# Up product of an encoder layer: groups of three tiles, two of them by seven products, and weight forms in pieces of 1024 columns

## The chip, the cores and the metric

The kernel runs on one core of a Trainium2 chip. A time is the device time of one execution in microseconds; the kernel before has a median of 783.61 us over 3 runs (783.21 to 783.69). The profile is one execution recorded by the hardware profiler. PE is TensorE (matmuls), PEld its weight loads, DVE VectorE, ACT ScalarE, POOL GpSimd, SP SyncE.

## The reference

One layer for 512 tokens of width 1024, in float32:

```python
x1 = x  + RMSNorm_post_mix( W_out( sig(a_ret) * W_ret_o(Retention(h)) + sig(a_sgu) * W_sgu_o(SGU(h)) ) )
y  = x1 + RMSNorm_post_ffn( ConvGatedMLP( RMSNorm_pre_ffn(x1) ) )

def _conv_gated_mlp(h, w_up, conv_w, conv_b, w_down):
    hid = h @ w_up                      # (512, 1024) @ (1024, 2 * 2816)
    hid = conv(hid, conv_w) + conv_b    # each channel by itself, 3 tokens
    a, b = jnp.split(hid, 2, axis=-1)
    return (jax.nn.gelu(a) * b) @ w_down
```

(`conv` stands for the reference's call of the library.) The change is mostly in `h @ w_up`, the up product.

## The kernel before

**Precision.** Every product is made of float32 values split into a high and a low part (`split`: ACT copies to a rounded type, DVE subtracts, L119). Three matmuls stand for one: high by high, high weight by low activation, low weight by high activation.

**The up product.** `w_up` has 2 x 2816 columns, which are 22 tiles of 128 channels of `a` with the 128 of `b` that belong to them. A tile computed whole is two blocks (`f_block`), one for `a` and one for `b`: 8 pieces of 128 rows, three matmuls of 512 columns (the tokens) each, 24 matmuls into one bank of PSUM. A tile by seven products (`Pair`) treats its 2 x 2 submatrices by a Strassen form: seven products of 12 matmuls of 256 columns (`product`, L926), 84 in place of 8 x 12. For these the weights are added in forms first (`w_form`: T1 to T4 from B11, B12, B21, B22), and so are the activations (S1 to S4, made once). `part1` makes four products (B11 and B21, then T1 by S1 and T2 by S2), `part2` one (T3 by S3), `part3` the last two (T4 and B22). They use three banks: the first product's bank is copied out by ACT (`copy(two(c0[:, T0]), o)`) before the fourth product is written to it, and ACT copies the fourth and fifth too; DVE adds the second, fifth's partner and last. The last is the subtraction at L976, which completes the tile.

Tiles 0 to 3 are whole. `COUPLES` are (4, 5) to (18, 19): the first tile of each by seven products, the second whole, one inside the other. 20 and 21 are whole. `tile_done` makes the convolution of a finished tile (`conv`: one ACT operation L1247, two of DVE, L1250 and L1254, for each of its two parts), then `gated` (GELU on ACT L1261, a product on DVE L1263), and after tiles 7, 9, 11, 13 and 17 the forms of the down product's activations (`down_forms`: `fs`, `fa`, `fh`, `fl`; some of their low parts come by an adding transfer on POOL's queue, L1273).

**Weights.** All weights lie in `wall`, in pieces of 128 x 1024 (512 KB). SP starts a piece's transfer to a `raw` tile (4 buffers), ACT and DVE split it into slots of the pool `w4` (9 buffers of 1088 columns). A whole block takes two slots, high and low; a form of a seven-product tile is 512 columns and has its high and low part in one slot. `units` lists the pieces in the order of use, `w_get` hands out the next and prepares those behind it while they fit in nine slots (`w_size`).

**The order.** Each engine executes its instructions in the order in which a scheduler put them when the program was built; it starts from the order in the code and from its own view of times, and may move an instruction past others. What waits for a semaphore holds up all that stands behind it on its engine.

The seven-product kind is also used for two other stages: the products U and G (four pairs each, order in `MIDDLE`) and four gated pairs (`gated_pair`). The pairs of those stages use the same `w_form`; for G and the gated pairs T2 and T4 are added by POOL (`eng`), else by DVE.

## Time and profile before

| | before |
|---|---|
| median of the runs | 783.61 us |
| span of the profiled execution | 782.6 us |
| busy PE / DVE / ACT / POOL | 774.5 / 639.5 / 485.2 / 103.5 us |
| matmuls | 5139 |
| transfers `raw<-wall` by SP's queue | 144, 512 KB each, 3.7 us from issue to landing |
| software queue (POOL's transfers) | 14.95 MB, 9.0% of 16 engines' span |

The profiled execution's own time is the span of 782.6 us, and what lies around the span in the runs is 783.61 - 782.6 = 1.0 us. The up product from its first couple is the stretch from about 490 to 639 us. The page divides the span into 40 slices of 19.6 us; busy tenths of an engine in each show which engine is full where:

```profile
PE   9999999999999999999999999999999999999996
DVE  6567987789789988877765679989999889886987
ACT  7555568688466766644454686657777568644542
POOL 0040001130021102033211200001111012200001
```

The up product's couples are slices 26 to 33.

### The profile page before, as it was taken

How to read it: one execution, taken by the hardware profiler on the slowest of the kernel's cores; microseconds unless marked ns; L12 is line 12 of the kernel's file. 1: busy time of each engine (PE TensorE's matmuls, PEld its weight loads, DVE VectorE, ACT ScalarE, POOL GpSimd, SP SyncE). 2: the span in 40 equal slices, each digit the busy share in tenths (PEclk: the TensorE clock that was granted, in tenths of full speed). 3: DMA queues.
4: the chain of work that ended last, by engine and by line, in shares of the span. 5: the costliest groups of instructions: out<-in, count | busy, mean ns of one | idle time of the engine just before them, and what ended most of it. 6: DMA issues, size and time to landing. Idle time of an engine off the chain costs nothing.

```text
span 782.6 us, 13472 instructions
## 1 busy us (share of the span) xinstructions
PE 774.5 (99%) x5139; PEld 720.7 (92%) x5139; DVE 639.5 (82%) x1093; ACT 485.2 (62%) x878; POOL 103.5 (13%) x132
## 2 busy tenths in 40 slices
PE   9999999999999999999999999999999999999996
PEld 8888998998999999999998998999999998999996
DVE  6567987789789988877765679989999889886987
ACT  7555568688466766644454686657777568644542
POOL 0040001130021102033211200001111012200001
PEclk9999999999999999999999999999999999999998
DMA  8783224453223233233459120435555375733344
GB/s 288 271 246 102 81 82 162 108 122 108 81 91 126 82 122 121 83 110 106 138 171 337 54 81 28 124 107 141 142 148 149 108 199 111 171 114 107 109 162 162
DMA packets 35889, 104.80 MB, mean 134 GB/s; under 512 B 4400, under 2 KB 6320, under 8 KB 35824
## 3 DMA queue, kind: packets, MB, share of 16 engines
q1 hardware_dynamic: 27936, 87.81, 34.0%
q0 software_dynamic: 7024, 14.95, 9.0%
q10 hardware_dynamic: 864, 1.18, 0.4%
q8 instruction: 40, 0.66, 0.4%
q14 instruction: 25, 0.20, 0.1%
HBM read 91.34 MB, written 4.19 MB: 122 GB/s over the span
## 4 chain that ended last, share of the span: by engine, by line
PE 92%; DVE 3%; DMA 3%; issue 1%; ACT 0%; POOLq 0%; DVEq 0%; POOL 0%; ACTq 0%
PE ps L926 24%; PE ps L300 12%; PE ps L302 12%; PE ps L301 12%; PE ps L1372 7%; PE ps L755 5%; PE ps L634 4%; PE ps L636 4%; PE ps L635 4%; DMA raw<-wall 3%; PE ps L1109 2%; PE ps L1108 2%; PE ps L1107 2%; DVE dl L119 1%; PE ps L997 1%
## 5 line engine op out<-in xcount | busy, mean ns | idle before, releaser
L119 DVE TENSOR_TENSOR wl<-raw,wh 128x1024 fp32r<-128x1024 f32 (+1 forms) x84 | 96.0, 1152 | 54.3 <-issue 19.1
L100 ACT ACTIVATE wf<-raw 128x512 fp32r<-128x512 f32 x140 | 85.6, 625 | 67.3 <-PE ps L301 19.4
L926 PE MATMUL ps<-sh,wf 128*128 128x256 f32 x640 | 117.4, 276 | 0.1
L119 DVE TENSOR_TENSOR wf<-raw,wf 128x512 fp32r<-128x512 f32 x140 | 107.0, 774 | 9.2 <-ACT wf L100 8.6
L926 PEld LDWEIGHTS ps<-sh,wf 128*128 128x128 f32 x640 | 101.9, 192 | 1.1 <-ACT sig L100 0.5
L100 ACT ACTIVATE wh<-raw 128x1024 fp32r<-128x1024 f32 (+2 forms) x88 | 84.8, 977 | 28.5 <-DMA raw<-wall 14.0
L300 PE MATMUL ps<-h2h,wh 128*128 128x512 f32 (+1 forms) x256 | 90.6, 354 | 0.0
L301 PE MATMUL ps<-h2l,wh 128*128 128x512 f32 (+1 forms) x256 | 90.4, 353 | 0.0
L302 PE MATMUL ps<-h2h,wl 128*128 128x512 f32 (+1 forms) x256 | 90.4, 353 | 0.0
L926 PE MATMUL ps<-sl,wf 128*128 128x256 f32 x320 | 88.0, 275 | 0.0
L926 PEld LDWEIGHTS ps<-sl,wf 128*128 128x128 f32 x320 | 61.4, 192 | 0.4
L1372 PE MATMUL ps<-dh,fh 128*128 128x256 f32 x216 | 59.6, 276 | 0.3 <-DVE yy L1409 0.3
L1372 PE MATMUL ps<-dl,fh 128*128 128x256 f32 x216 | 59.5, 275 | 0.0
L1372 PE MATMUL ps<-dh,fl 128*128 128x256 f32 x216 | 59.4, 275 | 0.0
L100 ACT ACTIVATE dh<-raw 128x768 fp32r<-128x768 f32 (+1 forms) x36 | 33.6, 950 | 33.8 <-DVE raw L231 15.2
L302 PEld LDWEIGHTS ps<-h2h,wl 128*128 128x128 f32 x256 | 48.6, 190 | 5.1
L301 PEld LDWEIGHTS ps<-h2l,wh 128*128 128x128 f32 x256 | 48.6, 190 | 4.5
L300 PEld LDWEIGHTS ps<-h2h,wh 128*128 128x128 f32 x256 | 48.6, 190 | 4.5
L926 PE MATMUL ps<-xh,wf 128*128 128x256 f32 x288 | 52.2, 275 | 0.0
L636 PE MATMUL ps<-wh,xl 128*128 128x512 f32 x128 | 48.5, 379 | 0.0
L635 PE MATMUL ps<-wl,xh 128*128 128x512 f32 x128 | 48.5, 379 | 0.0
L634 PE MATMUL ps<-wh,xh 128*128 128x512 f32 x128 | 48.5, 380 | 0.0
(343 smaller groups left out, 2171.6 us busy)
## 6 DMA issues: line engine op xcount, KB each, us to landing
raw<-wall SPq DMA_DIRECT2D x144, 512.0 KB, 3.7
x<-x SPq DMA_DIRECT2D x24, 256.0 KB, 6.0
fl<-gp POOLq DMA_DIRECT2D x12, 256.0 KB, 3.8
swap<-qkraw POOLq DMA_DIRECT2D x16, 128.0 KB, 4.8
x<-x POOLq DMA_DIRECT2D x8, 256.0 KB, 2.3
fl<-fs POOLq DMA_DIRECT2D x8, 256.0 KB, 4.3
xT<-xT SPq DMA_DIRECT2D x7, 256.0 KB, 5.0
xT<-xT POOLq DMA_DIRECT2D x4, 256.0 KB, 4.1
```

The costliest lines, as they stand in the source:

```text
L100: return nc.scalar.activation(out=o, in_=i, func=AF.Copy)
L119: low[0] = nc.vector.tensor_sub(lo, src, as32(hi)).ins
L300: nc.tensor.matmul(o, ah, bh, start=start, stop=False, skip_group_check=skip)
L301: nc.tensor.matmul(o, ah, bl, start=False, stop=False, skip_group_check=skip)
L302: pe_last[0] = nc.tensor.matmul(o, al, bh, start=False, stop=stop, skip_group_check=skip).ins
L634: nc.tensor.matmul(acc[t], xh[k][:, c], turns(wh[:, f]), start=k == 0, stop=False)
L635: nc.tensor.matmul(acc[t], xh[k][:, c], turns(wl[:, f]), start=False, stop=False)
L636: part_end[0] = nc.tensor.matmul(acc[t], xl[k][:, c], turns(wh[:, f]), start=False, stop=k == KD - 1)
L755: nc.tensor.matmul(bank[t], a_[:, c], turns(w_[:, f]), start=first and k == i == 0, stop=last and k == 3 and i == 2, skip_group_check=True,)
L926: self.last = nc.tensor.matmul(o, w_[:, c], a_, start=first and k == n == 0, stop=k == 3 and n == 2, skip_group_check=True,)
L1107: nc.tensor.matmul(o, ah, turns(bh), start=k == 0, stop=False)
L1372: nc.tensor.matmul(o, a_[:, c], turns(w_[:, f]), start=j == t == i == 0, stop=j == DP - 1 and i == 2 and n not in (M2, M3, M4), skip_group ...
```

## The change

**Groups.** `GROUPS` takes the place of `COUPLES`: (4, 5) and (6, 7) stay, then four groups of three tiles, (8, 9, 10) to (17, 18, 19). In a group of three the first and last tile are by seven products, the middle one whole. Ten tiles in all are by seven products (before eight), six in groups are whole (before eight).

**Order in a group of three.** First tile's `part1`; the middle tile's first block with the first tile's `part2` in its middle; first tile's `part3`, and `tile_done`; last tile's `part1`; middle tile's second block with the last tile's `part2` in its middle; `tile_done` of the middle tile; last tile's `part3`, and `tile_done`. In these blocks (`low_last`) the 16 matmuls with the weight's high part come first and the eight with its low part last; `part2` stands between the first 12 and the rest.

**Low part by an adding transfer.** For the middle tile of a group of three (unit "added", eight blocks) ACT copies the high part, then writes its negative to the low part's slot, and a transfer of 512 KB from `wall` on POOL's queue is added to it. There is no subtraction on DVE and the weight is read twice.

**Forms in pieces of 1024 columns.** In all pairs the seven units of 512 columns become "B1" (B11 and B21), "T12" and "T34" with 1024 columns and two slots each, and "B22" with 512 and one slot: three copies and three subtractions of 1024 and one each of 512 in place of seven of 512. T1, T2 and T3 are always added by DVE; only T4 is POOL's in G and the gated pairs. The weights' layout in `wall` is arranged to fit (`_two`, `_up`).

```diff
-COUPLES = [(i, i + 1) for i in range(4, 20, 2)]
+GROUPS = [(4, 5), (6, 7)] + [(i, i + 1, i + 2) for i in range(8, 20, 3)]
...
-    FORMS = ("B11", "B21", "T1", "T2", "T3", "T4", "B22")
+    FORMS = ("B1", "T12", "T34", "B22")
...
-            for a, b in COUPLES:
+            for a, b, *c in GROUPS:
                 pair = [(f, UP0 + 2 * a) for f in FORMS]
-                units += pair[:4] + [("blk", UP0 + 2 * b)] + pair[4:] + [("blk", UP0 + 2 * b + 1)]
+                b = [("added" if c else "blk", UP0 + 2 * b + n) for n in range(2)]
+                if c:
+                    last = [(f, UP0 + 2 * c[0]) for f in FORMS]
+                    units += pair[:2] + b[:1] + pair[2:] + last[:2] + b[1:] + last[2:]
+                else:
+                    units += pair[:2] + b[:1] + pair[2:] + b[1:]
...
+    def w_added(i):
+        raw = raw_tile()
+        nc.sync.dma_start(raw, wall[i])
+        hi, lo = slot("wh"), slot("wl")
+        copy(hi, raw)
+        nc.scalar.activation(out=lo, in_=as32(hi), func=AF.Copy, scale=-1.0)
+        nc.gpsimd.dma_start(lo, wall[i], accum_op=ALU.add)
+        return hi, lo
+
     def w_form(form, i):
 
-        if form == "B11":
-            a, b = raw_tile(), raw_tile()
+        eng = nc.vector if i < GATE0 or i >= UP0 else nc.gpsimd
+        if form == "B1":
+            a, b = w_raw["a"], w_raw["b"] = raw_tile(), raw_tile()
             nc.sync.dma_start(a, wall[i])
             nc.sync.dma_start(b, wall[i + 1])
-            w_raw["B11"], w_raw["B12"] = a[:, :S], a[:, S:]
-            w_raw["B22"], w_raw["B21"] = b[:, :S], b[:, S:]
-        elif form == "T1":
-            t = raw_tile()
-            w_raw["T1"], w_raw["T2"], w_raw["T3"], w_raw["T4"] = t[:, :S], t[:, S:], w_raw["B12"], t[:, S:]
-            nc.vector.tensor_add(w_raw["T1"], w_raw["B11"], w_raw["B12"])
-            nc.vector.tensor_add(w_raw["T3"], w_raw["B12"], w_raw["B22"])
-            eng = nc.vector if i < GATE0 or i >= UP0 else nc.gpsimd
-            eng.tensor_tensor(out=w_raw["T2"], in0=w_raw["T1"], in1=w_raw["B22"], op=ALU.add)
-        elif form == "T4":
-            eng = nc.vector if i < GATE0 or i >= UP0 else nc.gpsimd
-            eng.tensor_tensor(out=w_raw["T4"], in0=w_raw["T2"], in1=w_raw["B21"], op=ALU.add)
-        w = slot("wf", 0, 1088)
-        lo, hi = w[:, AT_64 : AT_64 + S], w[:, S + AT_192 : 2 * S + AT_192]
-        split(hi, lo, w_raw[form])
+            w_raw["B22"], w_raw["B12"] = b[:, :S], b[:, S:]
+            raw = a
+        elif form == "T12":
+            raw = w_raw["t"] = raw_tile()
+            nc.vector.tensor_add(raw[:, :S], w_raw["a"][:, :S], w_raw["B12"])
+            nc.vector.tensor_add(raw[:, S:], raw[:, :S], w_raw["B22"])
+        elif form == "T34":
+            raw = w_raw["a"]
+            nc.vector.tensor_add(raw[:, :S], w_raw["B12"], w_raw["B22"])
+            eng.tensor_tensor(out=raw[:, S:], in0=w_raw["t"][:, S:], in1=raw[:, S:], op=ALU.add)
+        if form == "B22":
+            w = slot("wf", 0, 1088)
+            lo, hi = w[:, AT_64 : AT_64 + S], w[:, S + AT_192 : 2 * S + AT_192]
+            raw = w_raw["B22"]
+        else:
+            hi, lo = slot("wf", AT_192), slot("wf", AT_64)
+        split(hi, lo, raw)
         return hi, lo
...
-        return 2 if u[0] in ("blk", "q", "t") or u[0][0] == "s" else 1
+        return 1 if u[0] == "B22" else 2
...
-    def f_block(ah, al, n, between=None):
+    def f_block(ah, al, n, between=None, low_last=False):
 
         wh, wl = w_get()
         o = ps()
+        if low_last:
+            parts_ = [(w_, a_, k) for k in range(n) for w_, a_ in ((wh, ah), (wh, al))] + [(wl, ah, k) for k in range(n)]
+            for i, (w_, a_, k) in enumerate(parts_):
+                if between and i == len(parts_) // 2:
+                    between()
+                pe_last[0] = nc.tensor.matmul(
+                    o, w_[:, k * P : (k + 1) * P], turns(a_[k]), start=i == 0, stop=i == len(parts_) - 1
+                ).ins
+            return o
...
-    couples = dict(COUPLES)
+    sizes = {g[0]: len(g) for g in GROUPS}
     i = 0
     while i < NF:
-        if i in couples:
+        if i in sizes:
             p = Pair(None, lambda: tmp("c"), (h2h, h2l, h2forms))
             p.part1()
-            o = [f_block(h2h, h2l, KD)]
-            p.part2()
-            o.append(f_block(h2h, h2l, KD, p.part3))
-            tile_done(i, p.t)
-            tile_done(i + 1, o)
-            i += 2
+            if sizes[i] == 2:
+                o = [f_block(h2h, h2l, KD)]
+                p.part2()
+                o.append(f_block(h2h, h2l, KD, p.part3))
+                tile_done(i, p.t)
+                tile_done(i + 1, o)
+            else:
+                o = [f_block(h2h, h2l, KD, p.part2, True)]
+                p.part3()
+                tile_done(i, p.t)
+                p = Pair(None, lambda: tmp("c"), (h2h, h2l, h2forms))
+                p.part1()
+                o.append(f_block(h2h, h2l, KD, p.part2, True))
+                tile_done(i + 1, o)
+                p.part3()
+                tile_done(i + 2, p.t)
+            i += sizes[i]
```

**Where instructions stand.** Line numbers of the changed kernel differ from those of the kernel before: its `conv` is L1280, L1283 and L1287 (before L1247, L1250, L1254), its gated product L1296 (before L1263), a pair's last subtraction L1009 (before L976), a second product's addition L978 (before L948), its negative copy L204 and its adding transfer L205.

DVE before, at a couple's end: `c_1100` is the pair's second half (its last subtraction is L976), `ps_1121` the whole tile's second block, `c_1136` the next couple's first product.

```order
L976 TENSOR_TENSOR c_1100_6415<-ps_1103_6418,c_1100_6415 128x256
L119 TENSOR_TENSOR wf_1119_6544<-raw_1108_6466,wf_1119_6544 128x512
L1254 SCALAR_TENSOR_TENSOR cv_1122_6602<-c_1099_6414,part_63,cv_1122_6602 128x511
L1250 SCALAR_TENSOR_TENSOR cv_1123_6606<-c_1100_6415,part_63,cv_1123_6606 128x511
L1250 SCALAR_TENSOR_TENSOR cv_1125_6613<-ps_1114_6496,part_63,cv_1125_6613 128x511
L119 TENSOR_TENSOR wf_1120_6548<-raw_1112_6489,wf_1120_6548 128x512
L1254 SCALAR_TENSOR_TENSOR cv_1123_6606<-c_1100_6415,part_63,cv_1123_6606 128x511
L1254 SCALAR_TENSOR_TENSOR cv_1125_6613<-ps_1114_6496,part_63,cv_1125_6613 128x511
L1263 TENSOR_TENSOR gp_1124_6611<-cv_1122_6602,cv_1123_6606 128x512
L1250 SCALAR_TENSOR_TENSOR cv_1126_6617<-ps_1121_6551,part_63,cv_1126_6617 128x511
L119 TENSOR_TENSOR wf_1141_6652<-raw_1109_6467,wf_1141_6652 128x512
L1254 SCALAR_TENSOR_TENSOR cv_1126_6617<-ps_1121_6551,part_63,cv_1126_6617 128x511
```

DVE of the changed kernel, at the end of the group (11, 12, 13): `c_1111` is tile 13's second half, `ps_1123` the second block of tile 12, `c_1143` tile 14's first product.

```order
L1283 SCALAR_TENSOR_TENSOR cv_1130_6535<-ps_1123_6479,part_63,cv_1130_6535 128x511
L1287 SCALAR_TENSOR_TENSOR cv_1130_6535<-ps_1123_6479,part_63,cv_1130_6535 128x511
L119 TENSOR_TENSOR wf_1128_6516<-raw_1116_6439,wf_1127_6515 128x1024
L1296 TENSOR_TENSOR gp_1131_6540<-cv_1129_6531,cv_1130_6535 128x512
L1009 TENSOR_TENSOR c_1111_6406<-ps_1114_6409,c_1111_6406 128x256
L1283 SCALAR_TENSOR_TENSOR cv_1132_6568<-c_1110_6405,part_63,cv_1132_6568 128x511
L119 TENSOR_TENSOR wf_1148_6607<-raw_1117_6440,wf_1148_6607 128x512
L1287 SCALAR_TENSOR_TENSOR cv_1132_6568<-c_1110_6405,part_63,cv_1132_6568 128x511
L1283 SCALAR_TENSOR_TENSOR cv_1133_6572<-c_1111_6406,part_63,cv_1133_6572 128x511
L978 TENSOR_TENSOR c_1143_6602<-ps_1146_6605,c_1143_6602 128x256
```

The pair's last subtraction stood ahead of the whole tile's convolution steps, and now stands behind them, behind a subtraction of 1024 columns and behind the whole tile's product.

ACT of the changed kernel at the same place: `wl_1126` is the next added block's negative copy, `c_1143` the copy of tile 14's first product out of its bank.

```order
L100 ACTIVATE wh_1125_6494<-raw_1124_6492 128x1024
L204 ACTIVATE wl_1126_6495<-wh_1125_6494 128x1024
L1280 ACTIVATE cv_1130_6535<-ps_1123_6479,part_63 128x512
L100 ACTIVATE wf_1127_6515<-raw_1116_6439 128x1024
L1294 ACTIVATE cv_1129_6531<-cv_1129_6531 128x512
L100 ACTIVATE c_1110_6405<-ps_1112_6407 128x256
L100 ACTIVATE wf_1148_6607<-raw_1117_6440 128x512
L1280 ACTIVATE cv_1132_6568<-c_1110_6405,part_63 128x512
L1280 ACTIVATE cv_1133_6572<-c_1111_6406,part_63 128x512
L100 ACTIVATE c_1143_6602<-ps_1145_6604 128x256
```

The negative copy stands ahead of the convolution's start of the block that has just ended, and the convolution's start of the pair's second half (`cv_1133`) ahead of the next tile's first copy.

POOL's queue in the changed kernel between two adding transfers of weights, where before the transfers of the down forms stood alone:

```order
L205 DMA wl_1096_6309<-wall 128x1024
L1306 DMA fl_1105_6391<-fs_1103_6385 128x512
L1306 DMA fl_1107_6396<-gp_987_5617 128x512
L1306 DMA fl_1109_6401<-gp_984_5606 128x512
L205 DMA wl_1126_6495<-wall 128x1024
```

Each adding transfer of a weight stands behind up to three of the down forms.

Over the whole program DVE has 1040 rows for 1082 before, ACT 786 for 827, PE 5121 for 5005; matmuls of the seven-product kind are 1848 for 1680.

49 lines of the change are left out of this document (26 added, 23 removed).

## The prediction

> **What bounds the kernel now.** I read the page's first part first, then the chain that ended last.
>
> ```profile
> span 782.6 us, 13472 instructions
> PE 774.5 (99%) x5139; PEld 720.7 (92%) x5139; DVE 639.5 (82%) x1093; ACT 485.2 (62%) x878; POOL 103.5 (13%) x132
> PE 92%; DVE 3%; DMA 3%; issue 1%; ACT 0%; POOLq 0%; DVEq 0%; POOL 0%; ACTq 0%
> ```
>
> TensorE is busy for 99% of the span and is 92% of the chain, so taking matmuls away can show in full, and any new wait of TensorE is paid in full. The waits of PE say how close the other engines come (columns: total us, times, longest):
>
> ```profile
> PE ps L402 <- PEq L1669: 0.8, 1, 0.8
> PE ps L1372 <- DVE yy L1409: 0.3, 1, 0.3
> ```
>
> Neither lies in the up product. There the stretches (PE, PEld, DVE, ACT, POOL busy, granted clock, DMA share, GB/s) read:
>
> ```profile
> core 0: us, PE busy (x) PEld busy (x) DVE busy (x) ACT busy (x) POOL busy (x), PEclk, DMA share, GB/s
> 530.00:570.00 40.00, 40.00 (x271) 37.42 (x271) 36.83 (x62) 28.92 (x56) 7.00 (x8) 1.00 0.54 141
> 570.00:610.00 40.00, 40.00 (x271) 37.42 (x270) 37.48 (x64) 29.95 (x54) 5.15 (x6) 1.00 0.57 148
> ```
>
> PE is busy for 40.00 of 40 us at a granted clock of 1.00; DVE for 92 and 94% of it and ACT for 72 and 75%. So DVE is the engine next to the bound, with some 3 us free in 40. The prices of matmuls come from the chain in order of time:
>
> ```profile
> 154.40 5.18 PE ps L755 x24
> 529.76 5.36 PE ps L926 x48
> 549.50 5.36 PE ps L926 x48
> 272.59 9.38 PE ps L926 x84
> 246.62 19.00 PE ps L926 x168
> ```
>
> 24 matmuls of 512 columns take 5.18 us, 0.2158 each; 48 of 256 columns take 5.36, 0.1117 each; a whole seven-product pair is the row of 84 in 9.38. Two couples begin 549.50 - 529.76 = 19.74 us apart, which is 84 x 0.1117 + 48 x 0.2158 = 19.74: no idle time at all inside a couple.
>
> **The change, part by part.**
>
> *Matmuls (certain).* Twelve tiles after the first eight (8 to 19) change from six couples to four triples: two more tiles by seven products, two fewer whole. That removes 96 matmuls of 512 columns, 96 x 0.2158 = 20.72 us, and adds 168 of 256 columns, 168 x 0.1117 = 18.77. **Term 1: -1.95 us.** A triple then has 2 x 9.38 + 48 x 0.2158 = 29.12 us of matmuls.
>
> *Work of DVE and ACT.* Start-to-start times are taken from a couple's start, which the next parts need too, first of ACT and then of DVE (start, us, engine, line, operation):
>
> ```profile
> 549.38 0.62 ACT L1261 ACTIVATE cv<-cv 128x512 f32<-128x512 f32 x1
> 549.90 0.61 ACT L100 ACTIVATE wf<-raw 128x512 fp32r<-128x512 f32 x1
> 550.42 0.76 ACT L1247 ACTIVATE cv<-ps,part 128x512 f32<-128x512 f32 x1
> 551.09 0.62 ACT L100 ACTIVATE wf<-raw 128x512 fp32r<-128x512 f32 x1
> 551.61 0.37 ACT L100 ACTIVATE c<-ps 128x256 f32<-128x256 f32 x1
> 551.87 1.05 ACT L100 ACTIVATE wh<-raw 128x1024 fp32r<-128x1024 f32 x1
> 552.82 0.63 ACT L1261 ACTIVATE cv<-cv 128x512 f32<-128x512 f32 x1
> ```
>
> ```profile
> 547.54 0.42 DVE L976 TENSOR_TENSOR c<-ps,c 128x256 f32<-128x256 f32 x1
> 549.14 0.74 DVE L1250 SCALAR_TENSOR_TENSOR cv<-c,part,cv 128x511 f32<-128x511 f32 x1
> 549.80 0.74 DVE L1250 SCALAR_TENSOR_TENSOR cv<-ps,part,cv 128x511 f32<-128x511 f32 x1
> 552.48 0.68 DVE L1263 TENSOR_TENSOR gp<-cv,cv 128x512 f32<-128x512 f32 x1
> 553.08 0.74 DVE L1250 SCALAR_TENSOR_TENSOR cv<-ps,part,cv 128x511 f32<-128x511 f32 x1
> 556.26 1.22 DVE L119 TENSOR_TENSOR wl<-raw,wh 128x1024 fp32r<-128x1024 f32 x1
> 557.40 0.42 DVE L1290 TENSOR_TENSOR fs<-fs,gp 128x256 f32<-128x256 f32 x1
> 557.73 0.69 DVE L119 TENSOR_TENSOR wf<-raw,wf 128x512 fp32r<-128x512 f32 x1
> ```
>
> DVE takes 1.14 us for 1024 columns (556.26 to 557.40), 0.60 for 512, 0.66 for a convolution step, 0.33 for 256; ACT 0.95 for 1024 (551.87 to 552.82), 0.52 for 512, 0.67 for a first convolution step. By these a couple costs DVE some 17.7 us (7 subtractions of 512, 2 of 1024, 4 form additions, 8 convolution steps, 2 products, 3 of 256, and its share of the down forms): 90% of 19.74. A triple costs it 2 x (3 x 1.14 + 0.60) + 8 x 0.62 + 12 x 0.66 + 3 x 0.60 + 6 x 0.33 + 1.65 = 26.4: 91% of 29.12. The added transfers take two subtractions off DVE and the additional pair puts its own on: even. ACT's forms go from 3.6 of 19.74 to 6.7 of 29.12 us, its whole blocks from 1.9 to 3.8, since each added block has two copies of 1024 where it had one, and its `c` copies from 4 to 8: with 0.3 for one of these, 10 points more, some 84% where the stretches showed 72 and 75. Neither becomes the bound by its sum, so this part costs nothing while queues run ahead; where they don't, the next two parts price it.
>
> *The adding transfers* are eight issues on POOL's queue, 512 KB each. The pool of weight slots has nine buffers, and a half triple needs 2 + 2 + 2 + 2 + 1 = 9, so the low part's slot is the one that the block before has just left: the negative copy can start only when that block's last low matmul is done. From there: 0.95 copy, then issue and landing. The nearest rows are the adding transfers from the weights earlier in the kernel, and the issues that POOL makes in this stage:
>
> ```profile
> raw<-wall POOLq DMA_DIRECT2D x2, 512.0 KB, 6.4
> fl<-gp POOLq DMA_DIRECT2D x12, 256.0 KB, 3.8
> L1273 POOL DMA_DIRECT2D fl<-gp x20: 853/868/1545, 500.7 to 673.8; - x20
> ```
>
> 0.95 + 0.87 + 6.4 = 8.2 us, and up to three issues of the down forms ahead of it on POOL, 3 x 0.87 = 2.6: 10.8. The eight low matmuls now come last in their block, 29.12 / 2 - 8 x 0.2158 = 12.8 us after the slot came free. **Hidden, with 2.0 to 4.6 us to spare; 0.** Without that cover each microsecond is paid eight times. A rule speaks against this part. The Trainium skill ("SBUF — State Buffer", section "SBUF: two separate sides") says that a DMA issued from GpSimd waits for its descriptors while VectorE holds the port that the two share, in a two-port mode. By that rule an engine 91% busy could hold these transfers back; the 3.8 us above were landed beside a DVE 92 to 94% busy, so the trace doesn't show it, and the sum by it is a rival below.
>
> *The new order at a triple's end.* Before, a pair's last products stood inside the second whole block: its last subtraction (L976) was at 547.54, 1.96 us before the couple's end at 549.50. The next pair's first product must be copied out of its bank (the `c` copy) before the fourth product takes it: the copy ended at 551.61 + 0.37 = 551.98, the fourth began at 549.50 + 36 x 0.1117 = 553.52, 1.54 us to spare. Now the last products follow the block, and the order of DVE's rows puts the whole tile's two last convolution steps, a subtraction of 1024 and a product ahead of that subtraction. Counted from the block's last matmul: negative copy on ACT to 1.0, convolution start (0.76) to 1.8, two steps to 3.2 (2 x 0.66, and a handover), subtraction to 4.4, product to 5.0, the pair's last subtraction (0.42) to 5.4, convolution start on ACT (0.82) to 6.3, `c` copy to 6.7. The fourth product is due 24 x 0.1117 + 36 x 0.1117 = 6.70 after the block. Spare: 0.0 instead of 1.54. At three ends (the last triple is followed by a whole tile) I take 0.3 us of wait each, for small lateness of two engines this full: 0.9. Ends: 0 if the last steps run earlier than this, and 1.0 each if one more ACT copy of 1024 comes in between.
>
> *Between a triple's two pairs* the same chain starts with the last subtraction: 0.47, convolution start 0.82, GELU 0.52, a weight copy 0.52, `c` copy 0.37 and handovers, about 2.9 of 4.0 us. That is enough, except where ACT runs behind. After tiles 7 and 13 the down forms' copies stand in the same half triple; before they took ACT 3.05 us in a row, from the first to the row after the last:
>
> ```profile
> 557.85 0.64 ACT L100 ACTIVATE fh<-fs 128x512 fp32r<-128x512 f32 x1 [1.53 <-DVE fs L1290]
> 560.90 0.61 ACT L100 ACTIVATE wf<-raw 128x512 fp32r<-128x512 f32 x1
> ```
>
> 3.05 - 1.1 = 1.9 is the worst at each; some of it is caught up in the 6 us between, so I take 0.4 each: 0.8, with ends 0 and 3.8. **Term 2: +1.7 us** (0 to 6.8, and below nothing it can't be, as no wait of PE stands there now).
>
> *Forms of 1024 columns in the other twelve pairs* (eight of them gated). Fewer, longer copies: 3 x 0.95 + 0.52 = 3.4 us of ACT for 7 x 0.52 = 3.6. The second addition goes from POOL to DVE in the gates, 0.69 for 1.68:
>
> ```profile
> 217.16 1.77 DVE L206 TENSOR_TENSOR raw<-raw,raw 128x512 f32<-128x512 f32 x1
> L206 DVE TENSOR_TENSOR raw<-raw,raw 128x512 f32<-128x512 f32 x8 | 6.6, 823 | 2.3 <-DMA raw<-wall 2.3
> L208 POOL TENSOR_TENSOR raw<-raw,raw 128x512 f32<-128x512 f32 x5 | 8.4, 1679 | 67.6 <-DMA raw<-wall 67.5
> ```
>
> One DVE addition took 1.77 us where others take 0.69. What PE can win is little: the row of 168 matmuls took 19.00 where 168 x 0.1117 = 18.77, 0.23 over. What it can lose is the longer first copy, 1.05 - 0.62 = 0.43, once or twice. **Term 3: 0** (-0.2 to +0.9).
>
> The sum is -1.95 + 1.7 + 0 = -0.25 us. The profiled span of 782.6 becomes 782.35; what lies around the span is 783.61 - 782.6 = 1.0 against the median of the runs, so the median becomes **783.4 us**.
>
> **The rivals.** A change below 0.2%, 1.57 us, can't be told from none here: "same" is 782.04 to 785.18.
>
> *Nothing of term 2 shows.* The queues absorb the new order, and the matmuls' gain comes through, with the 0.2 of term 3: 783.61 - 1.95 - 0.2 = 781.5, faster. For it: PE shows no wait in this stage, and ACT sat idle for 1.53 us at the row of 557.85 alone. Against it: the spare of 1.54 is gone by the order of the rows.
>
> *ACT's copies decide at every border: slower.* The place is the `c` copy at all seven borders from tile 8 on. If ACT reaches it one copy of 1024 late, 0.7 to 0.95 us of wait come at each: 783.61 - 1.95 + 7 x 0.7 = 786.6, or 788.3. The point from which it decides is 3.5 us of waits, 0.5 per border. For it: ACT's load grows by 10 points and DVE is at 91%. Against it: four of the seven borders have 1.1 to spare before any lateness.
>
> *The adding transfer is late.* If landing takes twice the 6.4 us, 0.95 + 0.87 + 12.8 = 14.6 against 12.8, 1.8 us are missing eight times: 783.61 - 1.95 + 14 = 796. For it only the rule above; against it 3.8 us in the same stage.
>
> *The change doesn't remove what it says.* PE has 5121 rows in the order for 5005, and 1848 matmuls of the seven-product kind for 1680; the arithmetic of term 1 stands on that, so I give it nothing.
>
> **How the numbers follow.** My forecast (no measurable change, 782.04 to 785.18) 0.45; nothing of term 2 shows 0.34; ACT's copies 0.18; late transfers 0.03. So faster 0.34, same 0.45, slower 0.21. Time 783.4. The range runs from 781.2 (all of terms 1 and 3, and 0.3 for the runs' own spread) to 786.4 (near the low price of the slower rival): about 0.1 is left out above and 0.1 below. The forecast's own range is 782.0 to 785.2.
>
> **What would show it.** Term 1: in the chain, two seven-product pairs and 48 matmuls of 512 columns from triple to triple, 29.12 us apart plus waits. Term 2: waits of PE for ACT's `c` copy, at L956, of 0.3 to 0.5 each at five borders; none means the first rival, 0.7 or more at each the second. The adding transfer: the group at L205, landing within 6.4 us, and no wait of PE for POOL's queue at L924. Term 3: the rows of 84 and 168 matmuls at 9.4 and 18.8. The forecast is wrong if the up product loses more than 3.5 us to waits, or none.

## The result, and the profile after

The changed kernel takes 788.96 us (median of 5 runs, 788.38 to 789.26) where the kernel before takes 783.61. The ratio is 1.0065, 95% interval 1.0054 to 1.0076: **slower by 5.3 us**, outside the range of the prediction (781.2 to 786.4) and on the side that had a chance of 0.21.

The first part of the page and its shares of the chain by engine, as shown of the kernel before:

```profile
span 787.4 us, 13540 instructions
PE 774.1 (98%) x5211; PEld 721.8 (92%) x5211; DVE 636.1 (81%) x1051; ACT 489.8 (62%) x838; POOL 99.8 (13%) x132
PE 52%; DVE 6%; ACT 5%; issue 2%; POOLq 0%; POOL 0%; DVEq 0%; ACTq 0%
```

PE's busy time hardly changed (774.5 before), the span grew by 4.8 us: what was saved in matmuls was given back as idle time, and more. The chain no longer runs through PE alone. The waits of PE (total us, times, longest) name the reason:

```profile
PE ps L956 <- ACT c L100: 2.8, 4, 1.2
PE ps L956 <- ACT u L100: 1.9, 2, 1.4
PE ps L419 <- PEq L1710: 0.8, 1, 0.8
PE ps L956 <- ACT sig L100: 0.3, 1, 0.3
```

Three of the four rows are one thing: a product (L956) that waits until ACT has copied the first product out of its bank. The copies `c` are the up product's, `u` and `sig` those of the U and G products, at 230 to 275 us.

To put numbers on stretches I use one measure throughout, worked out from PE's rows of the timeline: the time from one matmul's start to the next, less 0.2158 us (512 columns) or 0.1117 (256), added up over all gaps above 0.02 us. I call it **lost time**.

| lost time of PE, us | U, G and gated products | up product | all else |
|---|---|---|---|
| before | 0.92 | 0.00 | 5.20 |
| after | 3.47 | 4.77 | 4.12 |

So the U and G products lost 2.55 us more, the up product 4.77, the rest 1.08 less, and 1.95 of matmuls were saved: 4.29 us. With the stretch behind the last matmul, which is 0.57 us longer, that is the 4.86 by which the span grew (from 782.55 to 787.42).

Two more things of the prediction can be read off. The adding transfers landed later than assumed and still cost PE nothing (the group at L205: the issue, then the time from its start to the landing as minimum, median, maximum):

```profile
L205 POOL DMA_DIRECT2D wl<-wall x8: 857/862/923, 531.2 to 637.6; - x8
DMA to landing us min/median/max: 5.7/7.4/9.1
```

No row of PE's waits names POOL's queue. The landing is counted from the start of the issue, so that the 0.87 us in the prediction's sum is counted twice; but the cover was thinner than its 12.8 us, as the negative copy stood behind other rows on ACT and didn't start when its slot came free. The transfer issued at 610.09 landed at 619.22, 0.2 us ahead of the first matmul that needs it (619.43), and the one issued at 550.23 landed at 557.97, 0.5 us ahead (558.47), both after PE had waited about 1 us for ACT in the same half group.

The rule of the Trainium skill ("SBUF — State Buffer", section "SBUF: two separate sides") that the prediction set against this part is one for a VectorE in a two-port mode. The same section of the Trainium skill says that `tensor_tensor` has no such mode; VectorE's rows beside these transfers are TENSOR_TENSOR and SCALAR_TENSOR_TENSOR, and each issue took 0.86 us. That they are adding transfers isn't what took the longer time either: in a run below (mixed_noneg) plain transfers of the same size landed in 4.0, 6.9 and 8.3 us (minimum, median, maximum).

And the time around the span: the run with this profile took 789.26 us for a span of 787.4, and the other four runs 1.7 to 1.9 more than theirs. By that the profiled execution of the kernel before (782.6) was one of 784.4 us, 0.8 above its median, and the 1.0 us that the prediction put around the span was too small.

### The profile page after: what moved, and what is told of

The parts are those of the page before. It is cut to its first block, busy times and chain, and to the rows that moved or that the text cites. A ratio compares the mean times of both kernels' runs of the same rounds, so it can differ in the third digit from the quotient of the medians.

```text
span 787.4 us, 13540 instructions
## 1 busy us (share of the span) xinstructions
PE 774.1 (98%) x5211; PEld 721.8 (92%) x5211; DVE 636.1 (81%) x1051; ACT 489.8 (62%) x838; POOL 99.8 (13%) x132
## 4 chain that ended last, share of the span: by engine, by line
PE 52%; DVE 6%; ACT 5%; issue 2%; POOLq 0%; POOL 0%; DVEq 0%; ACTq 0%
PE ps L956 16%; PE ps L1416 11%; PE ps L317 5%; PE ps L319 5%; PE ps L318 5%; PE ps L924 3%; PE ps L1140 2%; PE ps L1142 2%; PE ps L1141 2%; PE ps L1432 2%; ACT wf L100 1%; DVE cv L1287 1%; DVE cv L1283 1%; ACT cv L1280 1%; DVE gp L1296 1%
## 5 line engine op out<-in xcount | busy, mean ns | idle before, releaser
L956 PE MATMUL ps<-sh,wf 128*128 128x256 f32 x704 | 131.3, 277 | 5.1 <-ACT c L100 2.8
L956 PEld LDWEIGHTS ps<-sh,wf 128*128 128x128 f32 x704 | 112.8, 192 | 8.0 <-ACT c L100 4.7
L119 DVE TENSOR_TENSOR wf<-raw,wf 128x1024 fp32r<-128x1024 f32 x88 | 101.2, 1152 | 13.3 <-ACT wf L100 11.7
L119 DVE TENSOR_TENSOR wl<-raw,wh 128x1024 fp32r<-128x1024 f32 (+1 forms) x72 | 80.8, 1132 | 36.9 <-ACT wh L100 16.6
L100 ACT ACTIVATE wf<-raw 128x1024 fp32r<-128x1024 f32 x88 | 82.8, 947 | 44.7 <-DVE raw L220 22.6
L956 PE MATMUL ps<-sl,wf 128*128 128x256 f32 x352 | 96.9, 275 | 0.0
L956 PEld LDWEIGHTS ps<-sl,wf 128*128 128x128 f32 x352 | 67.6, 192 | 0.4
L317 PE MATMUL ps<-h2h,wh 128*128 128x512 f32 (+1 forms) x160 | 54.2, 339 | 0.0
L318 PE MATMUL ps<-h2l,wh 128*128 128x512 f32 (+1 forms) x160 | 54.0, 338 | 0.0
L319 PE MATMUL ps<-h2h,wl 128*128 128x512 f32 (+1 forms) x160 | 54.0, 338 | 0.0
L956 PE MATMUL ps<-xh,wf 128*128 128x256 f32 x288 | 52.2, 276 | 0.0
L956 PEld LDWEIGHTS ps<-xh,wf 128*128 128x128 f32 x288 | 45.7, 192 | 0.2
L956 PE MATMUL ps<-h2h,wf 128*128 128x256 f32 x240 | 43.6, 276 | 0.0
L1416 PEld LDWEIGHTS ps<-dh,fh 128*128 128x128 f32 x216 | 41.5, 192 | 0.0
```

Source lines behind the costliest of these rows:

```text
L100: return nc.scalar.activation(out=o, in_=i, func=AF.Copy)
L119: low[0] = nc.vector.tensor_sub(lo, src, as32(hi)).ins
L317: nc.tensor.matmul(o, ah, bh, start=start, stop=False, skip_group_check=skip)
L318: nc.tensor.matmul(o, ah, bl, start=False, stop=False, skip_group_check=skip)
L319: pe_last[0] = nc.tensor.matmul(o, al, bh, start=False, stop=stop, skip_group_check=skip).ins
L956: self.last = nc.tensor.matmul(o, w_[:, c], a_, start=first and k == n == 0, stop=k == 3 and n == 2, skip_group_check=True,)
```

## The two places where the time went

**The U and G products.** The third and largest wait there is 1.4 us at 264.02. ACT's rows ahead of it:

```profile
256.60 0.37 ACT L100 ACTIVATE sig<-ps 128x256 f32<-128x256 f32 x1
259.88 1.08 ACT L100 ACTIVATE wh<-raw 128x1024 fp32r<-128x1024 f32 x1 [2.92 <-DMA raw<-wall]
260.98 1.28 ACT L1085 ACT_TABLE_LOAD   x1
262.28 0.63 ACT L1085 ACTIVATE u<-u 128x512 f32<-128x512 f32 x1
262.81 0.36 ACT L100 ACTIVATE sig<-ps 128x256 f32<-128x256 f32 x1
263.08 0.62 ACT L1085 ACTIVATE u<-u 128x512 f32<-128x512 f32 x1
263.60 0.37 ACT L100 ACTIVATE u<-ps 128x256 f32<-128x256 f32 x1
```

The copy that PE waits for is the last. It isn't late because ACT has much to do: ACT stood idle for 2.92 us at the copy of a whole block's weight, which hadn't landed, and all that stands behind it moved. In the kernel before the same row stood there without a wait, ahead of the same table load:

```profile
255.96 1.05 ACT L100 ACTIVATE wh<-raw 128x1024 fp32r<-128x1024 f32 x1
```

SP's queue tells why (start, duration of the issue), first before, then after:

```profile
225.53 0.33 SPq L176 DMA_DIRECT2D raw<-wall  x1
251.24 0.33 SPq L176 DMA_DIRECT2D raw<-wall  x1
```

```profile
228.49 0.33 SPq L181 DMA_DIRECT2D raw<-wall  x1
256.17 0.33 SPq L181 DMA_DIRECT2D raw<-wall  x1
```

The same two transfers of whole blocks (L176, now L181) are issued 3.0 and 4.9 us later. There are four raw buffers, and a transfer waits until a subtraction of DVE has read one and given it back (SP's waits from 220 to 280 us: total, times, longest; before, then after):

```profile
SPq L176 <- DVE wf L119: 9.1, 4, 4.0
```

```profile
SPq L181 <- DVE wf L119: 19.3, 3, 9.7
```

**The up product.** Ahead of the largest wait, 1.2 us before tile 10's fourth product, ACT has no gap worth the name for 10 us. Its rows, and PE's row behind them:

```profile
542.92 0.63 ACT L100 ACTIVATE fh<-fs 128x512 fp32r<-128x512 f32 x1 [0.75 <-DVE fs L1323]
543.58 0.63 ACT L1305 ACTIVATE fl<-fh 128x512 fp32r<-128x512 f32 x1
544.12 0.71 ACT L100 ACTIVATE fh<-gp 128x256 fp32r<-128x256 f32 x2
544.73 0.40 ACT L1305 ACTIVATE fl<-fh 128x256 fp32r<-128x256 f32 x1
545.04 0.40 ACT L100 ACTIVATE fh<-gp 128x256 fp32r<-128x256 f32 x1
545.34 0.71 ACT L1305 ACTIVATE fl<-fh 128x256 fp32r<-128x256 f32 x2
545.96 1.05 ACT L100 ACTIVATE wf<-raw 128x1024 fp32r<-128x1024 f32 x1
546.91 0.36 ACT L100 ACTIVATE c<-ps 128x256 f32<-128x256 f32 x1
547.17 1.05 ACT L100 ACTIVATE wh<-raw 128x1024 fp32r<-128x1024 f32 x1
548.12 0.80 ACT L1280 ACTIVATE cv<-c,part 128x512 f32<-128x512 f32 x1
548.82 1.05 ACT L204 ACTIVATE wl<-wh 128x1024 fp32r<-128x1024 f32 x1
549.77 1.04 ACT L100 ACTIVATE wf<-raw 128x1024 fp32r<-128x1024 f32 x1
550.72 0.81 ACT L1280 ACTIVATE cv<-c,part 128x512 f32<-128x512 f32 x1
551.43 0.61 ACT L1294 ACTIVATE cv<-cv 128x512 f32<-128x512 f32 x1
551.95 0.61 ACT L100 ACTIVATE wf<-raw 128x512 fp32r<-128x512 f32 x1
552.47 0.36 ACT L100 ACTIVATE c<-ps 128x256 f32<-128x256 f32 x1
```

```profile
552.88 0.38 PE L956 MATMUL ps<-sh,wf 128*128 128x256 f32 x1 [1.19 <-ACT c L100]
553.10 0.28 PE L956 MATMUL ps<-sl,wf 128*128 128x256 f32 x1
```

The down forms of tile 7 (`fh`, `fl`, 3.0 us), the negative copy (L204) and the form copies (`wf`) all stand ahead of the copy at 552.47. So here it is the work of ACT in a row, with another cause than in the U and G products. The wait after tile 13 (0.93 us) is of the same kind: from 603.38 to 612.77 ACT has no gap, but just before it had stood idle for 3.45 us, until DVE had made the first of the down forms:

```profile
603.38 0.63 ACT L100 ACTIVATE fh<-fs 128x512 fp32r<-128x512 f32 x1 [3.45 <-DVE fs L1323]
```

At the ends of the second and the third group (waits of 0.66 and 0.14 us) it is another thing: ACT stands idle until DVE has done the pair's last subtraction (L1009), and the copy comes behind that. At the second group's end:

```profile
596.46 0.81 ACT L1280 ACTIVATE cv<-c,part 128x512 f32<-128x512 f32 x1 [0.71 <-DVE c L1009]
597.18 0.36 ACT L100 ACTIVATE c<-ps 128x256 f32<-128x256 f32 x1
```

This is the chain that the prediction walked. The block's last matmul gave way to the next at 590.14 and the copy ended at 597.54, 7.4 us later, where the walk had 6.7 and the fourth product was due after 6.70.

## The experiments

The kernel "with short early forms" (label mixed) has forms of 512 columns in the U, G and gated pairs and all else as changed; most experiments on the up product build on it.

| kernel | time, us (runs' range) | lost in U, G, gated | lost in up |
|---|---|---|---|
| forms_only | 786.95 (786.84 to 788.77) | 3.34 | 0.89 |
| mixed | 786.41 (785.24 to 787.17) | 0.49 | 4.72 |
| groups_512 | 801.07 (800.53 to 804.28) | 0.70 | 22.7 |
| bursts | 787.73 (787.44 to 788.50) | 3.26 | 4.40 |
| forms_tmp4 | 791.18 (one run) | 2.78 | 5.52 |
| forms_raw5_tmp4 | 791.66 (790.32 to 792.70) | 0.32 | 5.44 |
| mixed_split | 785.65 (785.04 to 786.00) | 0.34 | 4.33 |
| mixed_later | 787.93 (786.94 to 789.19) | 0.34 | 5.82 |
| mixed_noburst | 803.78 (802.57 to 804.06) | 0.34 | 3.17 |
| mixed_noneg | 784.84 (784.25 to 786.63) | 0.34 | 4.20 |
| mixed_noneg_noburst | 802.00 (one run) | 0.60 | 0.38 |
| mixed_spread | 786.06 (785.94 to 788.21) | 0.34 | 5.00 |
| mixed_spread_b | 785.07 (784.24 to 785.79) | 0.51 | 3.70 |
| mixed_dvecopy | 791.25 (790.31 to 791.49) | 0.54 | 8.11 |
| two_groups | 788.85 (787.26 to 790.51) | 0.44 | 5.21 |
| two_groups_spread | 786.24 (785.26 to 789.08) | 0.43 | 7.30 |

The kernel before, run beside them, took 783.3 to 783.5.

Lost time is that of the one profiled execution. Its time lay within 1.2 us of the kernel's median, but 3.2 us above it for groups_512 and 2.8 above for two_groups_spread, and 1.6 below for two_groups. So differences of less than about 1 us in lost time say nothing by themselves.

### The change in its parts

The forms alone (forms_only):

```diff
-GROUPS = [(4, 5), (6, 7)] + [(i, i + 1, i + 2) for i in range(8, 20, 3)]
+GROUPS = [(i, i + 1) for i in range(4, 20, 2)]
```

> The forms of 1024 columns alone; the couples (4, 5) to (18, 19) of the kernel before stay. Theory of two costs (the longer forms cost the U and G products about 2.7 us, the order of the groups of three costs the up product about 3.6 us): 783.6 + 2.7 = 786.3 us, waits of PE at 240 to 275 us as in the changed kernel, none above 0.3 us in the up product. Rival, the longer forms are free and the waits at 240 to 275 come from something else in the change: 783.4 to 783.8. Second rival, the longer forms are also what makes the up product late: waits of 1 us or more in the up product, 787 or above.

Ratio 1.0054 (1.0040 to 1.0068). The U and G products lose what they lose in the changed kernel, 3.34 of 3.47; the up product 0.89, with no wait above 0.3 us. Both rivals fall.

The groups with short early forms (mixed: the seven old units and `w_form` for all pairs ahead of the up product):

> The changed kernel with forms of 512 columns in the U, G and gated pairs alone (as before), 1024 in the up product. Theory of two costs: the 2.7 us at 240 to 275 go and nothing else: 789.0 - 2.7 = 786.3 us, the up product's waits as in the changed kernel. Rival, the waits at 240 to 275 don't come from the forms: 789.

Ratio 1.0035 (1.0022 to 1.0047). As the theory had it: 0.49 and 4.72. The two losses are apart: each part of the change brings its own.

The groups of three with forms of 512 columns everywhere (groups_512):

> The groups of three with their adding transfers alone; forms of 512 columns everywhere as in the kernel before. Theory of two costs: no waits at 240 to 275 us, and the up product's waits of about 3.6 us stay against 1.95 us of matmuls saved: 785.3 us. Rival, the long copies of 1024 columns are what delays ACT's queue in the groups too: the waits in the up product fall below 1 us and the time to 782.5 or less.

Ratio 1.0233 (1.0215 to 1.0251), and neither said so: the up product loses 22.7 us. ACT's waits in the up product begin with a row that the changed kernel has at 0.6 us:

```profile
ACT wf L100 <- DMA raw<-wall: 18.5, 9, 3.9
```

With these forms in groups of three the transfers of weights are late as well. Not all of the 22.7 us are waits: behind three of them, at 597, 628 and 665 us, the granted clock was halved for 3.4 us (0.66 on average from 597 to 602, 0.72 from 627 to 633 and from 664 to 670), and each matmul took twice its time, some 5 us in all. So the groups do better with forms of 1024 columns, and the U and G products with 512; why the transfers are late here was not followed up.

### The U and G products: a raw buffer more

A fifth raw buffer didn't fit beside the rest, so two work buffers made room for it; forms_tmp4 has the fewer work buffers without the raw buffer.

```diff
-        return sb.tile(list(shape), F32, tag="tmp", bufs=6, name=nm(n))
+        return sb.tile(list(shape), F32, tag="tmp", bufs=4, name=nm(n))
...
-        return sb.tile([P, 1024], F32, tag="raw", bufs=4, name=nm("raw"))
+        return sb.tile([P, 1024], F32, tag="raw", bufs=5, name=nm("raw"))
```

> The kernel with the forms of 1024 columns alone (couples as before), with five raw buffers for the weights' transfers where it has four, and room made for it by four small work buffers (`tmp`) where it has six. Theory: the waits of 2.5 us in the U and G products come from the weights' transfers, which start 3 to 5 us later than before since a piece of 1024 columns gives its raw buffer back later, so that ACT stands at a weight copy ahead of the first product's copy. With a buffer more these transfers start earlier: PE's waits at 230 to 275 us fall below 0.6 us, and the last matmul comes 2 us earlier unless the smaller `tmp` costs elsewhere. Rival: the longer copies themselves hold ACT's queue; the waits at 235, 252 and 262 us stay at 2.5 us.

> The forms of 1024 columns alone, with four raw buffers and four small work buffers (`tmp`) where it has six: the control for the run with five raw buffers. Theory (the fifth raw buffer, not the fewer work buffers, took PE's waits out of the U and G products): they are 2.5 us or more again at 230 to 275 us. Rival: below 1 us here too; then the work buffers changed the order there and the raw buffers are not shown to be the cause.

The fewer work buffers cost the up product 5.5 us in both, so the times say nothing; the stretch in question does. With four raw buffers ACT's costliest wait at 220 to 280 us is again the transfer, and PE waits for its copy:

```profile
ACT wh L100 <- DMA raw<-wall: 5.9, 2, 3.2
PE ps L956 <- ACT u L100: 1.6, 2, 1.2
```

With five, PE has no wait in the stretch and loses 0.32 us, less than the 0.92 of the kernel before; the whole blocks' transfers start at 223.63 and 247.22, earlier than in the kernel before.

The raw buffers are the cause here, and not the work buffers: a buffer comes back later, the next transfer starts later, ACT stands at its copy, and PE behind ACT. What makes the buffer come back later is not shown. The subtraction that frees it is a short one of 512 columns (at 255.46, the transfer at 256.17; before at 250.50 and 251.24), so that not its own length but its place behind longer pieces, or the two slots that a form of 1024 columns now has to wait for, may have moved it.

### The up product: moving the work

The down forms elsewhere (bursts, on the changed kernel as it is):

```diff
-            if i in (7, 9, 11, 13, 17):
+            if i in (5, 8, 11, 14, 17):
```

> The changed kernel with the down forms made after tiles 5, 8, 11, 14 and 17 (in each group of three after its first tile) where it has 7, 9, 11, 13 and 17. In the changed kernel no wait above 0.6 us followed the forms after 11 and 17, and the waits of 1.4, 0.5 and 0.9 us followed those after 7, 9 and 13. Theory (ACT's eight copies for the down forms, standing shortly ahead of a border, make the next tile's first copy late): these three go, 789.0 - 2.5 = 786.5 us; the wait at the end of the second group (0.65) stays. Rival (the chain at the borders is too long by itself, wherever the down forms stand): 788.5 to 789.3.

787.73 is between the two. The waits after tiles 7, 9 and 13 (1.4, 0.5, 0.9 us) go as the theory said, and the one at the second group's end, which should have stayed, falls from 0.66 to 0.19. Three new ones of 0.8, 1.0 and 1.0 come at 558, 589 and 619 us, ahead of the sixth product, which waits for the copy of the fifth: the down forms take their wait along.

The middle tile's end behind the pair's last products (mixed_later):

```diff
-                tile_done(i + 1, o)
                 p.part3()
+                tile_done(i + 1, o)
                 tile_done(i + 2, p.t)
```

> The kernel with forms of 512 columns in the U, G and gated pairs and the groups of three (786.4 us), but the middle tile's convolution is written behind the last tile's last two products, so that the pair's last subtraction needn't stand behind it on DVE. Theory of the chain at a group's end (negative copy, convolution, subtraction, product, then the pair's last subtraction): the waits of 0.5 and 0.7 at the group ends (567 and 594 us) go, those of 1.3 and 0.9 between two pairs of a group stay: 785.2 us. Rival (ACT's amount of work decides, not the order): the group ends keep their waits, or others take their place; 786 or above.

Both group ends lost their wait for the first copy (0.52 to nothing, 0.66 to 0.06), as the theory said, and the wait after tile 13 fell from 0.93 to 0.38. But others took their place: 0.3 and 0.4 at the fifth product of tile 11 and the sixth of tile 13, and 1.0 and 1.2 at 624 and 643 us. The rival's second half is what happened.

DVE in place of ACT for the low part (mixed_split):

```diff
-                b = [("added" if c else "blk", UP0 + 2 * b + n) for n in range(2)]
+                b = [("blk", UP0 + 2 * b + n) for n in range(2)]
```

> The kernel with forms of 512 columns in the U, G and gated pairs and the groups of three (786.4 us), but the middle tile's low part by DVE's subtraction, as all others, in place of ACT's negative copy and the adding transfer. Theory (ACT is the full engine at the borders: it runs without a gap for 9.9 us ahead of the worst wait): with 0.95 us less of ACT in each half group PE's waits in the up product fall from 4.7 us to about 2.5, 784.2 us. Rival (DVE, which then has 98% of a group's time to do, takes over): waits of 8 us or more, 790 or above.

4.33 us lost for 4.72, and 0.8 us less by the medians (785.65 for 786.41): neither. The adding transfer with its negative copy costs, within about 1 us, as much as a subtraction on DVE.

The copy of the first product on DVE (mixed_dvecopy):

```diff
-            copy(two(c0[:, T0]), o)
+            (nc.vector.tensor_copy(out=two(c0[:, T0]), in_=o) if self.h is not xh else copy(two(c0[:, T0]), o))
```

> The kernel with forms of 512 columns in the U, G and gated pairs and the groups of three (786.4 us), but the first product of the up product's pairs is copied out of its bank by DVE, not ACT. It then stands behind other instructions: DVE's. Theory (the wait is the position behind ACT's copies for the weights and the down forms, while DVE at the worst border, 542 to 553 us, has gaps): the waits at 548 and 609 us fall to half or less; new ones of 0.3 to 0.7 at the groups' ends, where DVE's row of convolution steps stands ahead; 785.5 us. Rival (any in-order queue this full is late by as much): 4 us of waits or more remain, 786 or above.

8.1 us lost. PE now waits for DVE: `DVE c L1010: 3.5, 8, 1.5`. The rival holds: it is no better in the other queue.

The fourth product later, with the same work (mixed_spread, and mixed_spread_b with the down forms after 5, 8, 11, 14 and 17):

```diff
-                o = [f_block(h2h, h2l, KD, p.part2, True)]
+                o = [f_block(h2h, h2l, KD, {8: p.fourth, 16: p.part2}, True)]
```

> The kernel with forms of 512 columns in the U, G and gated pairs and the groups of three (786.4 us), but in a group of three the fourth product stands behind the first 8 matmuls of the middle tile's block and the fifth behind 16 of the 24, where the fourth followed the third at once and the fifth stood behind 12. The same work on every engine; only the copy of the first product has 8 x 0.2158 = 1.73 us more until it is due, and the fourth's 0.86 less. Theory (the copy misses its due time at the borders by 0.5 to 1.4 us, and what misses it isn't carried on): the waits at 548, 594 and 609 us go and 1 to 1.5 us are left of 4.7: 783.0 us. Rival (ACT is behind by the amount of its work, so that each later copy is late too): the waits move to the fifth and sixth products, 785.5 or above.

> As the run with the spread products, and the down forms made after tiles 5, 8, 11, 14 and 17, each in a group of its own. Theory of due times: each group then has one set of the down forms and the later due time takes it in, no wait above 0.5 us, 782.3 us, faster than the kernel before by the matmuls saved less the 0.7 us or so that the kernel's other stages differ by. Rival: the set moved to a group's middle makes the fifth product's copy late, 784 or above.

Lost: 5.00 and 3.70, so that both rivals hold. In the first the waits at 594 and 609 us go and the one at 548 shrinks to 0.4, but that of tile 11 grows from 0.5 to 1.1, and new ones of 0.3, 0.3 and 1.0 come at later products of tiles 13 and 14. In the second two waits of 0.9 us stand ahead of the last products of tiles 10 and 13, behind the down forms. The second is the best form of the groups that was found, ratio 1.0020 (1.0011 to 1.0029), still slower than the kernel before.

### The up product: taking work away

> The kernel with forms of 512 columns in the U, G and gated pairs and the groups of three (786.4 us), but no down forms before tile 19; eight are then made after tiles 19 to 21. Theory (the down forms' eight or so copies on ACT are what makes the first product's copy late in the groups): PE's waits between 520 and 640 us fall from 3.5 us to below 1; what the forms cost at the end isn't what this run is for, and the whole may be slower. Rival (the borders' chain is too long without them too): 2 us or more of waits stay in that stretch.

```diff
-            if i in (7, 9, 11, 13, 17):
-                down_forms(len(dforms))
-        elif len(dforms) < EAGER:
-            down_forms(len(dforms))
+            return
+        while len(dforms) < EAGER - (NF - 1 - i):
+            down_forms(len(dforms))
```

Three waits of 1.45, 0.54 and 0.49 are there, one at each group's end, 2.5 us of them (3.2 lost in all): the rival. The waits elsewhere are gone. So the down forms aren't the whole cause.

> The kernel with forms of 512 columns in the U, G and gated pairs and the groups of three (786.4 us), without ACT's negative copy of the middle tile: the low part is a plain transfer of the weight itself, so a part of the computation is left out (the low part is not the low part). DVE, the transfers and the order of products stay. Theory (ACT's queue with 0.95 us less in each half group reaches the first product's copy in time): the waits in the up product fall from 4.7 us to 2 or less, 783.7 us or less. Rival (the chain over DVE and ACT at the borders decides, in which this copy is one of eight links): 3.5 us or more stay.

```diff
-        nc.scalar.activation(out=lo, in_=as32(hi), func=AF.Copy, scale=-1.0)
-        nc.gpsimd.dma_start(lo, wall[i], accum_op=ALU.add)
+        nc.gpsimd.dma_start(lo, wall[i])
```

(The low part is left out: the transfer brings the whole weight in its place.) 4.20 lost: the rival again, though by the medians the kernel is 1.6 us faster than mixed (784.84 for 786.41). Of the waits, 0.9, 0.5, 1.0 and 0.9 us, only the second stands at a group's end; the others are new, ahead of the last products of tiles 8, 13 and 14.

> The same without the negative copy, and no down forms before tile 19 (without the negative copy alone left in, that made 3.2 us of waits in the up product, three of them at the groups' ends). Theory: with both gone no wait above 0.4 us is left between 520 and 640 us; then these two together are the cause. Rival: the groups' ends still wait 0.5 us or more each; then the order of the last products behind the block is enough by itself. The whole time isn't what this run is for.

With both away nothing is lost between 520 and 640 us (the 0.38 of the table lie at 494, in the first couple). The stretch, in the columns of the prediction's, first with both (mixed), then without both:

```profile
520.00:640.00 120.00, 117.22 (x858) 110.19 (x857) 103.30 (x163) 90.52 (x145) 19.03 (x22) 1.00 0.66 162
```

```profile
520.00:640.00 120.00, 120.00 (x883) 114.46 (x882) 101.52 (x151) 73.78 (x110) 4.29 (x8) 1.00 0.45 152
```

ACT is busy for 73.8 of 120 us, in place of 90.5; DVE is as busy as ever (101.5 for 103.3), with 25 matmuls more done. **The negative copies and the down forms are between them the cause**, and each has its own waits: without the down forms those at the groups' ends are left, where the negative copy is the first link of the chain; without the negative copies most of those that are left stand behind the down forms' copies. One of the two alone leaves 3.2 to 4.2 us of the loss, both gone leave 0.38.

It isn't ACT's load as such. Over the same 120 us ACT is busy for 83.3 us in the kernel before, which loses nothing there, for 83.6 in mixed_noneg and for 79.3 in mixed_noburst, which both lose. Nor is ACT alone shown to be the cause: with the down forms go DVE's additions, 1.65 us each, for which ACT waits ahead of its copies (3.45 us above), and the groups' ends wait for a chain through DVE. Which engine's share matters more was not taken apart. More than six work buffers were not tried either, though with four (forms_tmp4) every couple from the second on loses about 0.6 us.

### Fewer groups

Groups of three only for tiles 14 to 19, with the down forms after 5, 7, 9, 11 and 13 (two_groups), and with the later fourth product (two_groups_spread):

```diff
+GROUPS = [(i, i + 1) for i in range(4, 14, 2)] + [(14, 15, 16), (17, 18, 19)]
```

> Groups of three only at the end, (14, 15, 16) and (17, 18, 19), with forms of 1024 columns there alone; all other pairs as in the kernel before, and the down forms after tiles 5, 7, 9, 11 and 13, outside the groups. One tile more by seven products than before: 48 x 0.2158 - 84 x 0.1117 = 0.98 us of matmuls saved. Theory (the negative copies and the down forms together are the cause, the first alone costs 0.5 to 1.4 at a group's end): one group end is left that can wait, 0.5 to 0.8 us with what follows it: 783.5 - 1.0 + 0.7 = 783.2 us. Rival (each border of a group waits whatever stands beside it): three borders of 0.8: 784.9 or above.

> The same two groups with the fourth product behind 8 and the fifth behind 16 of the block's matmuls. Theory: with the down forms outside, the 1.73 us of later due time takes in the one group end that is left, and no wait remains: 783.5 - 1.0 = 782.5 us, faster than the kernel before by 0.1%. Rival: the fifth product's copy, whose due time is 0.86 us nearer, waits in its place, 783.2 or above.

5.2 and 7.3 lost, from two groups (1.7 of the 7.3 in 3.4 us at half the granted clock, from 619.8 on). The down forms after tile 13 were not outside: their last copies ran into the first group and stood there, waiting for an adding transfer of their own, ahead of the copy that PE waits for:

```profile
604.04 0.64 ACT L100 ACTIVATE fh<-gp 128x512 fp32r<-128x512 f32 x1 [1.53 <-DMA fl<-fs]
607.61 0.63 ACT L1333 ACTIVATE fl<-fh 128x512 fp32r<-128x512 f32 x1 [1.04 <-DMA fl<-gp]
610.34 0.37 ACT L100 ACTIVATE c<-ps 128x256 f32<-128x256 f32 x1
```

So neither theory was tested as meant. No kernel here beats the one before.

## Why the prediction was wrong, point by point

Between the forecast of -0.25 us and the 5.35 that came lie 5.6 us: term 2 was 3.1 too small and term 3 2.55.

- *What bounds the kernel.* Right: PE, with every new wait paid in full. But it named DVE as next to the bound, by its 92 and 94%. ACT, at 72 and 75% before, was the one that PE came to wait for. Its load rose less than the 10 points of the prediction, to 78 and 80% (DVE 89 and 88%):

```profile
530.00:570.00 40.00, 38.81 (x279) 36.53 (x278) 35.42 (x57) 31.39 (x53) 7.03 (x9) 1.00 0.61 148
570.00:610.00 40.00, 39.15 (x291) 36.53 (x290) 35.26 (x58) 32.03 (x53) 9.28 (x11) 1.00 0.72 167
```

  That isn't full, and yet in a row of 10 us ahead of a copy it was.
- *Term 1, -1.95 us.* It holds as far as the runs can show it: the profile has 5211 matmuls for 5139, 72 more, which is 168 - 96, and without the negative copies and the down forms nothing is lost between 520 and 640 us at the same 0.2158 and 0.1117 per matmul. (The 116 rows more in the order of rows, 5121 for 5005, that the prediction rested on are not that number.)
- *The adding transfers, 0.* Right, but with luck: with 0.2 us to spare at the worst, not 2.0 to 4.6, and that behind a wait of PE in the same half group.
- *Term 2, +1.7 us (0 to 6.8).* **The mechanism was right, the size wrong: 4.77.** The step that failed is the choice of a small part of what was worked out. The places were the foreseen ones, 1.36 and 0.93 us after the down forms of 7 and 13 where 0.4 each was taken, 0.52, 0.66 and 0.14 at the three group ends where 0.3 each was taken, and 0.27 in the first couple, which no term had. The worst that the same chains gave was 1.9 and 1.0: half to three quarters of it came in four places, since ACT, once it had begun on the forms, had no gap to catch up in. What wasn't in the sum at all: the first matmul behind each wait takes twice its time (552.88 to 553.10 us above), 0.1 us each.
- *Term 3, 0 (-0.2 to +0.9).* **This step failed.** It priced the longer copies and the addition moved to DVE, and saw too little wait in the rows before. It put the wait for the weights' transfers at nothing: it didn't ask when a raw buffer comes back, and so when the next transfer starts. That moved by 3 to 5 us, and cost PE 2.55.
- *The time around the span.* 1.8 us, not 1.0, for the profiled execution of before was 0.8 above the median of its runs. Since the sum was made against that execution and then moved by the difference, this did no harm to the forecast.
- *The rivals.* "ACT's copies decide at every border" had the price nearly right (786.6 to 788.3) for half the reason: four borders, not seven, and the rest from the U and G products. It deserved more than 0.18: the order of the rows had shown the spare time gone, and nothing measured spoke for halving what was worked out.

## What to carry to other kernels

When an engine's queue is executed in order, look at what stands ahead of the one short instruction that the bound engine waits for, over the last 10 us, not at the engine's busy share; and when the walk says that the spare time is gone, don't cut the worst case to a quarter unless a row shows where the rest will be caught up. For a longer piece in a ring of buffers, ask when the buffer comes back and which transfer waits for it: where the prediction saw a copy grow by 0.43 us, transfers started 3 to 5 us later. A saving of 0.25% in the full engine's work is small beside one or two such waits, so the other engines' rows need as much care as its own.

## What the runs showed of the hardware beyond this

The adding transfers of 512 KB took 5.7 to 9.1 us to land (median 7.4) where two of them earlier in the kernel took 6.4; plain ones in their place took 4.0 to 8.3 (median 6.9, mixed_noneg). Behind a product's first matmul after a wait the next began 0.22 us later, not 0.11. After some waits of PE the granted clock was halved for 3.4 us: in groups_512 after the waits of 3.1, 2.5 and 2.5 us at 593, 624 and 662 us, in two_groups_spread after one of 2.3 at 617, but not in groups_512 after one of 2.4 at 571, nor in two_groups after one of 3.7 at 607.
